# The last recurrence head's stores on GpSimd's queue, eight places for the state's loads, two gates stored as sigmoids, squares in two buffers

## The chip, the cores and the metric

The kernel runs on one core of a Trainium2 chip. A core has four compute engines that the kernel uses side by side: TensorE (PE in the profile, with its weight loads as PEld), VectorE (DVE), ScalarE (ACT) and GpSimd (POOL). A fifth, SyncE (SP), only issues transfers here. Each engine works through its own queue in order, and waits on semaphores where an instruction needs what another engine or a transfer has not yet delivered. The metric is the device time of one execution in microseconds; of several executions the median counts.

## The reference, cut to what matters

One layer of a hybrid backbone over 1024 tokens of width 1024, with 256 context tokens: an adaLN-modulated norm, one combined projection, three token mixers (windowed attention `a`, global attention `b` with normed heads, a bidirectional recurrence `c`), each lifted to the model's width and merged by sigmoid gates, an output projection, and a gated MLP with a depthwise convolution.

```python
aq, ak, av, bq, bk, bv, cq, cf, cb, ci, cg, gates = jnp.split(h @ w_in, split_at, axis=-1)
...
bq = rms_norm(heads(bq, B_HEADS), qn)          # squares, sums, pow(-0.5)
bk = rms_norm(heads(bk, B_KV_HEADS), kn)
...
def merge_branches(ya, yb, yc, gates, w_branch, w_out):
    B_, L = ya.shape[:2]
    ys = jnp.stack([ya, yb, yc], axis=2)
    up = jnp.einsum('blnw,nwd->blnd', ys, w_branch)
    g = jax.nn.sigmoid(gates.reshape(B_, L, N_BRANCH, -1))
    return jnp.sum(g * up, axis=2) @ w_out
```

## The kernel before

All matmuls run on operands that are split into a high and a low part: a product is three matmuls (high by high, high by low, low by high, in an order that each line fixes). ACT casts the high part (`wh`, `T1h`), and DVE subtracts it to get the low part (`wl`, `T1l`). Weights pass through three buffers each of `wr`, `wh` and `wl`.

**Order.** A scheduler places the instructions of each engine, by the order of the program and by priorities (`tc.high_priority`, with an offset for weights and for some steps). What stands ahead of what on an engine is fixed when the program is built. A tile of a pool with one or a few buffers waits for the release of what lay there before.

**The stages that the change touches, in order of time:**

- *The recurrence's last head.* `hgrn_head` is run for four heads. Its `norm` (L1512) squares the head's output on ACT, sums on DVE, takes the power on GpSimd (L1519), and leaves a `turn` (L1522) for later, which transposes (L1525), multiplies by the output gate into `ys` (L1527) and stores it to `y_d` (L1529).
- *The first three gates.* `gate_unit` (L569) multiplies a gate's weights with the state `H` (24 matmuls of 128x512 for each half), copies the result to a tile on ACT (L585) and stores it to `gate_d` (L586). The list `gates` begins with (2,0), (2,1), (1,7). The first runs in the recurrence's pool and calls the two late turns; the other two run in the pool `p3`, in tiles of tag `c` (five buffers, L658).
- *`h_sums` (L660).* It reads the normed state back from `h_d` in eight loads of 512 KB (L666) into `c` tiles, forms four differences on DVE (L669) and splits each into high and low: `T1` to `T4`. A pair of products is then computed with seven block products instead of eight (`pair`, L705): `q0` on a quarter of `H`, `q1` on `T1`, `q2` on `T2`, `q3` on a quarter of `H`, `q4` on `T3`, `q5` on a quarter, `q6` on `T4`. The weights of `q1` to `q4` are sums that DVE makes (L722).
- *Token pairs and gate groups.* `tok_pair` (L840) computes two projections in token-major order, 48 matmuls of 128x256 for each block product; `gate_group` (L751) does four gates, 24 matmuls of 128x512 for each. Two PSUM tiles alternate between the block products; ACT drains `q0`, `q1`, `q2` and `q6` by copies (L870, L780), DVE adds `q3` and `q4` (L785, L875). The elementwise work on a finished projection is queued in `behind` and is called between later matmuls: for branch `b` a square on ACT (L822), a sum on DVE (L824), a scaling (L825), a power on GpSimd (L826), a product (L827), and the rotation (L805 to L810).
- *Attention's end and the merge.* Attention's last steps are matmuls, exponentials on ACT (L1779) and splits (L1664, L1665). `merge_up` (L1794) then makes three passes over the branches (`j` = 0, 1, 2 for `c`, `a`, `b`), eight units `i` each: 24 matmuls (L192 to L194) into `br`, a load of the gate `sgt` (L1822), a sigmoid on ACT (L1823), and the product and sum on DVE (L1826 to L1837). The first units of pass 0 (br20, br21) are placed into attention's end. In passes 1 and 2 a generator `mod_rest` (L593) adds one step to each unit: a load of 512 KB of `w_mod` into a single buffer (L599) and a multiply-add on DVE (L603); after eight of them it transposes the sum (L609, `pm`) and reduces it. The output projection (`wo_half`) follows with the same kind of step.

Names in the profile: `tmt` a token pair's PSUM tile, `g` a gate group's, `ct` and `cg` what they are drained into, `ch` a tile of `h_sums`, `st`, `sg` and `wr` raw weights and their sums, `xm` the merged result, `macc` the sum of `mod_rest`, `wmr` its load.

## Time and profile before

| what | us |
|---|---|
| median of three runs (lowest to highest) | 2078.73 (2076.67 to 2080.57) |
| the profiled execution's own time | 2079.55 |
| its span in the profile | 2077.8 |
| PE busy in the span | 2019.6 |
| DVE, ACT and POOL busy | 1500.8, 1042.1 and 260.4 |
| granted TensorE clock, mean | 0.990 |

The span begins with the program's first instruction and ends with its last; 1.75 us of the execution lie around it. A row of the timeline names the start, the time, the engine, the line, the operation, what it writes and reads, its shape and how many alike are merged; brackets at the end give how long the engine had been idle just before, and what released it. A row of the waits names who waited for whom, the sum, how many times, and the longest.

### The profile page before, as it was taken

To read this page: it belongs to the slowest core of one execution; us is meant where nothing else is said; L and a number is where in the kernel's file an instruction comes from. 1 tells how busy PE (TensorE), PEld (TensorE's weight loads), DVE (VectorE), ACT (ScalarE), POOL (GpSimd) and SP (SyncE) were. 2 spreads that over 40 slices of the span, in tenths; PEclk is the share of its full clock that TensorE was granted. 3 is DMA by queue.
4 is the path that set the end of the run, shared out by engine and by line. 5 is a ranking of instruction groups with operands and counts; after the bars stand their busy time and mean duration, and the time that the engine had idled before them with its cause. 6 is when DMAs were issued, how large, how long until landed. Compare 5 with 4: busy or idle time off the path is not lost.

```text
span 2077.8 us, 29535 instructions
## 1 busy us (share of the span) xinstructions
PE 2019.6 (97%) x11309; PEld 1683.9 (81%) x11309; DVE 1500.8 (72%) x2268; ACT 1042.1 (50%) x1749; POOL 260.4 (13%) x229
## 2 busy tenths in 40 slices
PE   8999999979999999999999899999999999999997
PEld 5888888869897788878888688788888888888886
DVE  3846656665756788678888757898767777779964
ACT  3533323332233877688887733346444544444442
POOL 0000000000011222100000000010333244300001
PEclk9999999989999999999999999999999999999998
DMA  9610111154535211211100475782222222268722
GB/s 370 220 46 31 42 51 33 50 177 131 179 115 181 87 55 54 81 45 32 36 24 24 142 244 194 234 292 87 88 82 82 86 77 82 90 227 307 257 69 82
DMA packets 121790, 248.62 MB, mean 120 GB/s; under 512 B 10608, under 2 KB 51440, under 8 KB 120624
## 3 DMA queue, kind: packets, MB, share of 16 engines
q1 hardware_dynamic: 121552, 246.47, 35.8%
q8 instruction: 89, 1.46, 0.3%
q14 instruction: 53, 0.43, 0.1%
q0 software_dynamic: 96, 0.26, 0.0%
HBM read 196.88 MB, written 49.81 MB: 119 GB/s over the span
## 4 chain that ended last, share of the span: by engine, by line
PE 61%; DVE 3%; DMA 2%; ACT 2%; issue 1%; POOL 0%; SPq 0%; DVEq 0%; POOLq 0%; ACTq 0%
PE pp L1660 5%; PE dn L1252 3%; PE dn L1254 3%; PE dn L1253 3%; PE po L1646 3%; PE po L1647 3%; PE up L1117 3%; PE up L1119 2%; PE up L1118 2%; PE gz L193 2%; PE gz L192 2%; PE gz L194 2%; PE upc L1119 2%; PE upc L1118 2%; PE upc L1117 2%; PE upd L1119 2%
## 5 line engine op out<-in xcount | busy, mean ns | idle before, releaser
L1665 DVE TENSOR_TENSOR pl<-pp,ph 128x512 fp32r<-128x512 f32 x236 | 159.3, 688 | 27.8 <-ACT ph L1664 23.3
L168 ACT CAST wh<-wr 128x1024 fp32r<-128x1024 f32 x71 | 74.6, 1051 | 188.1 <-PE wo L193 33.8
L1664 ACT CAST ph<-pp 128x512 fp32r<-128x512 f32 x236 | 135.2, 588 | 31.8 <-PE pp L1660 29.6
L169 DVE TENSOR_TENSOR wl<-wr,wh 128x1024 fp32r<-128x1024 f32 x71 | 88.1, 1240 | 78.4 <-ACT wh L168 77.7
L1252 PE MATMUL dn<-ac,wh 128*128 128x512 f32 (+2 forms) x311 | 119.3, 384 | 1.3 <-DVE xt L1260 1.2
L1253 PE MATMUL dn<-ac,wh 128*128 128x512 f32 (+2 forms) x311 | 119.3, 384 | 0.5 <-DVE ac L640 0.5
L1254 PE MATMUL dn<-ac,wl 128*128 128x512 f32 (+2 forms) x311 | 119.1, 383 | 0.0
L1646 PE MATMUL po<-ph,VHL 128*128 128x512 f32 x236 | 105.3, 446 | 1.1 <-ACT ph L1664 0.8
L192 PE MATMUL gz<-hh,wh 128*128 128x512 f32 x256 | 103.9, 406 | 0.5 <-ACT gs L585 0.5
L194 PE MATMUL gz<-hh,wl 128*128 128x512 f32 x256 | 102.5, 400 | 0.0
L193 PE MATMUL gz<-hl,wh 128*128 128x512 f32 x256 | 101.5, 397 | 0.0
L1647 PE MATMUL po<-pl,VHL 128*128 128x512 f32 x236 | 98.9, 419 | 0.0
L192 PE MATMUL br<-yh,wh 128*128 128x512 f32 x192 | 76.1, 398 | 3.4 <-DVE xm L1826 3.4
L639 ACT CAST wh<-wr 128x1024 fp32r<-128x1024 f32 (+1 forms) x38 | 38.6, 1018 | 79.5 <-issue 24.8
L1660 PE MATMUL pp<-ident,plat 128*128 128x128 f32 x512 | 77.1, 274 | 0.2 <-DVE pl L1665 0.2
L193 PE MATMUL br<-yl,wh 128*128 128x512 f32 x192 | 76.3, 398 | 0.4 <-DVE yl L1807 0.4
L999 ACT ACTIVATE u<-c,cw 128x1024 f32<-128x1024 f32 x38 | 47.3, 1246 | 58.0 <-DVE c L1154 30.0
L1660 PEld LDWEIGHTS pp<-ident,plat 128*128 128x128 f32 x512 | 62.3, 141 | 16.9 <-DVE pl L1665 2.3
L194 PE MATMUL br<-yh,wl 128*128 128x512 f32 x192 | 75.5, 395 | 0.0
L640 DVE TENSOR_TENSOR wl<-wr,wh 128x1024 fp32r<-128x1024 f32 (+1 forms) x38 | 44.7, 1178 | 41.9 <-ACT wh L639 41.9
L1252 PEld LDWEIGHTS dn<-ac,wh 128*128 128x128 f32 x311 | 58.4, 188 | 13.0 <-DVE xt L1260 1.0
L1253 PEld LDWEIGHTS dn<-ac,wh 128*128 128x128 f32 x311 | 58.4, 188 | 12.2 <-DVE ac L640 1.0
(1538 smaller groups left out, 6318.2 us busy)
## 6 DMA issues: line engine op xcount, KB each, us to landing
wr<-in_w_up SPq DMA_DIRECT2D x44, 512.0 KB, 3.6
wr<-in_w_cm SPq DMA_DIRECT2D x40, 512.0 KB, 3.8
wmr<-in_w_mod SPq DMA_DIRECT2D x32, 512.0 KB, 4.7
wr<-in_w_dn SPq DMA_DIRECT2D x30, 512.0 KB, 4.4
b<-act_d SPq DMA_DIRECT2D x25, 512.0 KB, 6.2
sgt<-gate_d SPq DMA_DIRECT2D x24, 512.0 KB, 4.4
wr<-in_w_tm SPq DMA_DIRECT2D x23, 512.0 KB, 3.7
act_d<-u SPq DMA_DIRECT2D x22, 512.0 KB, 2.6
```

The source lines that it names most:

```text
L192: T.matmul(psl, wh[:, k, c], hh[:, k0 + k, cols], start=s, stop=False)
L193: T.matmul(psl, wh[:, k, c], hl[:, k0 + k, cols], start=False, stop=False)
L194: T.matmul(psl, wl[:, k, c], hh[:, k0 + k, cols], start=False, stop=e)
L1119: T.matmul(psl, w[1][:, c], h[0][:, k], start=False, stop=e, **on)
L1252: T.matmul(z, w[0][:, c], h[0], start=s, stop=False, **on)
L1253: T.matmul(z, w[0][:, c], h[1], start=False, stop=False, **on)
L1254: T.matmul(z, w[1][:, c], h[0], start=False, stop=e, **on)
L1646: T.matmul(po, vv, ph, start=n == 0, stop=False)
L1647: T.matmul(po, vv, pl, start=False, stop=n == len(kts) - 1)
L1660: T.transpose(pp[:, h], PT(h, n), ident)
L1664: A.copy(ph, pp)
L1665: V.tensor_tensor(out=pl, in0=pp, in1=ph.bitcast(F32), op=ALU.subtract)
```

## The change

Five things, in one diff:

1. `gate_unit` takes a place, an issuer and a function. The first gate (2,0) goes to a tile of the recurrence's pool (tag F1), (2,1) and (1,7) to the tags `hsq` and `cs` of `p3`, each of one buffer. The three gates' six stores, and the last head's two `y_d` stores, are issued by GpSimd. Gates (2,0) and (2,1) are stored as sigmoids.
2. `h_sums` reads into eight separate places: five `c` tiles and the tags `t12`, `tbk` and `tbq`. On SP's queue no store stands between its loads any more: after `st02`'s load come ch000, ch010, ch002, ch012, ch110, ch112, ch100 and ch102 in a row, and the rotation's table `cs` behind them. Before, the two `y_d` stores stood ahead of `st02`, and gate stores, weight loads and the table among the eight.
3. The squares of branch `b` alternate between the buffers `hsq` and `cs`.
4. In the merge, `mod_rest` yields once more before its transposes.
5. The first two units of the merge (br20, br21) multiply by the stored sigmoid without an ACT step, and that product has a higher priority. The ACT program then has one table load at the first remaining sigmoid, where it had three.

```diff
-        def gate_unit(pool, n, i, mode, whole=None):
+        def gate_unit(pool, n, i, mode, place=None, by=SP, func=None):
...
-                gs = whole[:, hf] if whole is not None else pool.tile([P, 512], F32, tag="gs", name=f"gs{n}{i}{hf}", bufs=2)
-                A.copy(gs, z)
-                SP.dma_start(gate_d[n, i][:, hf * 512:hf * 512 + 512], gs)
+                if place is None or isinstance(place, tuple):
+                    gs = pool.tile([P, 512], F32, name=f"gs{n}{i}{hf}",
+                                   **(dict(tag=place[hf], bufs=1) if place else dict(tag="gs", bufs=2)))
+                else:
+                    gs = place[:, 0, hf * 512:hf * 512 + 512]
+                if func is None:
+                    A.copy(gs, z)
+                else:
+                    A.activation(gs, z, func)
+                by.dma_start(gate_d[n, i][:, hf * 512:hf * 512 + 512], gs)
...
-        def mod_rest(pool, js, bufs):
+        def mod_rest(pool, js, bufs, gap=False):
...
+                if gap:
+                    yield
                 for hf in range(2):
                     pm2 = bank("a", f"pm2{j}{hf}")
...
-            for j, _ in enumerate(gate_unit(c1, *gates[0], "mm")):
+            for j, _ in enumerate(gate_unit(c1, *gates[0], "mm", c1.tile([P, 2, L], F32, tag="F1", name="g0"), G, AF.Sigmoid)):
...
-                    f[a, b, k] = ctile(f"h{a}{b}{k}")
+                    if (a, b) == (1, 1) or a == 0 and b * k != 2:
+                        f[a, b, k] = ctile(f"h{a}{b}{k}")
+                    else:
+                        f[a, b, k] = p3.tile([P, 2, 512], F32, name=f"ch{a}{b}{k}", bufs=1,
+                                             tag={(1, 2): "t12", (0, 0): "tbk", (0, 2): "tbq"}[b, k])
...
-                for _ in gate_unit(p3, *gates[x], "mm", ctile(f"g{x}")):
+                for _ in gate_unit(p3, *gates[x], "mm", ("hsq", "cs"), G, AF.Sigmoid if x == 1 else None):
...
-                        sq = p3.tile([P, nb, nh, 64], F32, tag="hsq", name=f"hsq{nm}", bufs=1)
+                        sq = p3.tile([P, nb, nh, 64], F32, tag="cs" if u < 2 and t // nb % 2 else "hsq",
+                                     name=f"hsq{nm}", bufs=1)
...
-            merge_up(tc, nc, mp, ins, gate_d, y_d, xm, half, w_unit, gemm_cm, mm2, mod_rest(mq, (0, 1), 1))
+            merge_up(tc, nc, mp, ins, gate_d, y_d, xm, half, w_unit, gemm_cm, mm2, mod_rest(mq, (0, 1), 1, True))
...
-            SP.dma_start(y_d[2, h][:, sl], ys)
+            (G if h == CH - 1 else SP).dma_start(y_d[2, h][:, sl], ys)
...
+                lead = j == 0 and i < 2
                 s = mp.tile([P, L], F32, tag="sgt", name=f"sgt{n}{i}")
                 SP.dma_start(s, gate_d[n, i])
-                A.activation(s, s, AF.Sigmoid)
+                if not lead:
+                    A.activation(s, s, AF.Sigmoid)
                 zf = z.rearrange("p a b -> p (a b)")
                 if j == 0:
-                    V.tensor_tensor(out=mg[i], in0=zf, in1=s, op=ALU.mult)
+                    with tc.high_priority(offset=YPRIO if lead else 0):
+                        V.tensor_tensor(out=mg[i], in0=zf, in1=s, op=ALU.mult)
```

The scheduler's order changes with it. First place: DVE, in the first token pair, around the low half of `q2`'s weights, `wl45` (`wl43` belongs to `q1`, `wl47` to `q3`). Before:

```order
L640 TENSOR_TENSOR wl43_3683<-st02_3621,wh43_3682 128x1024
L669 TENSOR_TENSOR ch000_3577<-ch010_3579,ch000_3577 128x1024
L722 TENSOR_TENSOR st02_3621<-st02_3621,wr44_3736 128x1024
L640 TENSOR_TENSOR T1l_3456<-ch000_3577,T1h_3455 128x1024
L722 TENSOR_TENSOR wr46_3793<-wr46_3793,st02_3621 128x1024
L640 TENSOR_TENSOR wl45_3740<-st02_3621,wh45_3739 128x1024
```

Of the change, the last twelve rows up to the one behind `wl45`; `wl43` stands six rows above the first of them, and the five between are T1l, ch002, st02, ch000 and T1l:

```order
L686 TENSOR_TENSOR ch010_3583<-ch110_3595,ch010_3583 128x1024
L649 TENSOR_TENSOR T2l_3449<-ch000_3581,T2h_3448 128x1024
L686 TENSOR_TENSOR ch002_3588<-ch112_3603,ch002_3588 128x1024
L649 TENSOR_TENSOR T3l_3453<-ch010_3583,T3h_3452 128x1024
L686 TENSOR_TENSOR ch012_3590<-ch112_3603,ch012_3590 128x1024
L649 TENSOR_TENSOR T2l_3449<-ch002_3588,T2h_3448 128x1024
L686 TENSOR_TENSOR ch000_3581<-ch100_3611,ch000_3581 128x1024
L649 TENSOR_TENSOR T3l_3453<-ch012_3590,T3h_3452 128x1024
L686 TENSOR_TENSOR ch002_3588<-ch102_3616,ch002_3588 128x1024
L649 TENSOR_TENSOR T4l_3455<-ch000_3581,T4h_3454 128x1024
L649 TENSOR_TENSOR wl45_3744<-st02_3625,wh45_3743 128x1024
L649 TENSOR_TENSOR T4l_3455<-ch002_3588,T4h_3454 128x1024
```

`wl45` was the fifth operation after `wl43`; now it is the sixteenth, behind all of `h_sums` but the last step.

Second place: ACT, in the second gate group, around the copies that drain its PSUM tiles (`cg26` from `g260` and `g261`, for `q0`, `q1` and `q2` in this order) and the squares `hsq`. Before:

```order
L822 ACTIVATE hsq102_5247<-ct1011_4805 128x512
L780 COPY cg2611_5259<-g260_5201 128x1024
L639 CAST wh103_5361<-wr102_5357 128x1024
L822 ACTIVATE hsq110_5296<-ct1021_5199 128x512
L780 COPY cg2622_5308<-g261_5202 128x1024
L639 CAST wh105_5395<-sg26_5203 128x1024
L639 CAST wh107_5428<-wr106_5425 128x1024
L822 ACTIVATE hsq112_5330<-ct1021_5199 128x512
L780 COPY cg2612_5355<-g260_5201 128x1024
```

And of the change:

```order
L840 ACTIVATE hsq110_5300<-ct1021_5203 128x512
L797 COPY cg2611_5263<-g260_5205 128x1024
L648 CAST wh103_5365<-wr102_5361 128x1024
L840 ACTIVATE hsq112_5334<-ct1021_5203 128x512
L797 COPY cg2622_5312<-g261_5206 128x1024
L648 CAST wh105_5399<-sg26_5207 128x1024
L648 CAST wh107_5432<-wr106_5429 128x1024
L797 COPY cg2612_5359<-g260_5205 128x1024
```

Each square has moved up by one place: a drain that followed one square now follows the next, and the last drain, `cg2612`, has none ahead of it.

Third place: DVE, at the beginning of the merge, around the first products `xm0` and `xm1` (`wl126` is the low half of a later unit's weights). Before:

```order
L169 TENSOR_TENSOR wl126_11883<-wr126_11880,wh126_11882 128x1024
L1826 TENSOR_TENSOR xm0_11650<-br20_11694,sgt20_11719 128x1024
L1826 TENSOR_TENSOR xm1_11651<-br21_11723,sgt21_11748 128x1024
L601 TENSOR_SCALAR macc0_11999<-wmr00_12000,scc_83 128x1024
L1826 TENSOR_TENSOR xm2_11652<-br22_11758,sgt22_11783 128x1024
```

And of the change:

```order
L1847 TENSOR_TENSOR xm0_11654<-br20_11698,sgt20_11723 128x1024
L1847 TENSOR_TENSOR xm1_11655<-br21_11726,sgt21_11751 128x1024
L169 TENSOR_TENSOR wl126_11885<-wr126_11882,wh126_11884 128x1024
L608 TENSOR_SCALAR macc0_12001<-wmr00_12002,scc_83 128x1024
L1847 TENSOR_TENSOR xm2_11656<-br22_11760,sgt22_11785 128x1024
```

The two products stand ahead of `wl126`, which waits for a cast that waits for br21's last matmul. Further on, DVE's order in the first and second pass keeps its shape: `macc0`'s sixth step stands ahead of `yl02`, `xm7` and `yl03` (low halves of branch `a`'s input), in both kernels.

More of the change, by code (lines that the diff above doesn't have):

```diff
@@ L654, in build @@
             hb = {(a, b): [p[:, a * KQ:(a + 1) * KQ, (t1, t2)[b]] for p in H] for a in range(2) for b in range(2)}
-            ht = {n: [hs_.tile([P, KQ, LH], F32R, tag=f"T{n}{p}", name=f"T{n}{p}") for p in "hl"] for n in (4, 3, 2, 1)}
+            ht = {n: [hs_.tile([P, KQ, LH], F32R, tag=f"T{n}{p}", name=f"T{n}{p}") for p in "hl"] for n in (2, 1, 3, 4)}
+            p3.tile([P, 512], F32, tag="hsq", name="hsq", bufs=1)
+            p3.tile([P, 512], F32, tag="cs", name="cs0", bufs=1)
+            p3.tile([P, 1024], F32, tag="s", name="s0", bufs=1)
             def ctile(nm):
```

## The prediction

> **What bounds the kernel now.** I read the page's first part, then PE's waits, then timelines and windows around the longest of them.
>
> ```profile
> span 2077.8 us, 29535 instructions
> ...
> PE 2019.6 (97%) x11309; PEld 1683.9 (81%) x11309; DVE 1500.8 (72%) x2268; ACT 1042.1 (50%) x1749; POOL 260.4 (13%) x229
> ```
>
> ```profile
> PE tmt L861 <- ACT ct L870: 9.8, 1, 9.8
> ...
> PE g L770 <- ACT cg L780: 4.3, 2, 3.7
> PE br L192 <- DVE xm L1826: 3.4, 1, 3.4
> ...
> PE sbl L1772 <- ACT plat L1779: 2.1, 1, 2.1
> PE pm L609 <- DVE macc L603: 1.8, 1, 1.8
> ...
> PE tmt L861 <- ACT T1h L639: 1.5, 1, 1.5
> ...
> PE br L193 <- DVE yl L1807: 0.4, 1, 0.4
> ```
>
> PE is the bound: all its idle time is 58 us. The change goes at five waits of this list: 9.8 and 1.5 (first token pair), 4.3 (second gate group), 2.1 (attention's end), 3.4 and 1.8 (merge). What each is worth depends on what is late next there, so I go through the stages in order, against the profiled execution (2079.55 us: the span and 1.75 us around it). It lies 0.8 above the median of the three runs shown.
>
> **First token pair.**
>
> ```profile
> 430.15 1.73 SPq L666 DMA_DIRECT2D ch<-h_d  x3
> ...
> 454.48 2.72 SPq L666 DMA_DIRECT2D ch<-h_d  x2
> ...
> 460.57 0.36 SPq L666 DMA_DIRECT2D ch<-h_d  x1
> ```
>
> ```profile
> 464.26 1.01 ACT L870 COPY ct<-tmt 128x1024 f32<-128x1024 f32 x1
> ```
>
> ```profile
> 439.85 0.28 PE L861 MATMUL tmt<-wh,hh 128*128 128x256 f32 x1
> ...
> 465.32 0.58 PE L861 MATMUL tmt<-wh,T2h 128*128 128x256 f32 x1 [9.76 <-ACT ct L870]
> ...
> 472.88 0.28 PE L861 MATMUL tmt<-wh,hh 128*128 128x256 f32 x1
> ...
> 478.64 0.28 PE L861 MATMUL tmt<-wh,T3h 128*128 128x256 f32 x1
> ```
>
> These are the starts of q0, q2, q3 and q4. The last h_d load is issued at 460.57; ACT's casts wait for such loads, and the copy that frees q2's PSUM tile stands behind them. An undisturbed product takes 478.64 - 472.88 = 5.76 us; q2 took 7.56, so the clock that was low after the long wait cost 1.8. Without any wait q4 would start at 439.85 + 4 x 5.76 = 462.9, which is 15.8 earlier.
>
> With eight places, and without stores ahead of them, the loads are no longer what is late: in the new order they are out by the time at which the first one goes out now, some 430. Late next is DVE.
>
> ```profile
> 435.46 1.23 DVE L640 TENSOR_TENSOR wl<-st,wh 128x1024 fp32r<-128x1024 f32 x1 [1.42 <-ACT wh L639]
> ...
> 442.56 1.22 DVE L640 TENSOR_TENSOR wl<-st,wh 128x1024 fp32r<-128x1024 f32 x1
> ...
> 463.19 1.22 DVE L640 TENSOR_TENSOR T2l<-ch,T2h 128x1024 fp32r<-128x1024 f32 x1
> 464.33 1.22 DVE L640 TENSOR_TENSOR T3l<-ch,T3h 128x1024 fp32r<-128x1024 f32 x1
> ```
>
> The first row is wl43, the second wl45. Such operations follow each other every 1.14 us (last two rows). wl43 waits for a cast that waits for PE, so I leave it at 435.46. wl45 is now the sixteenth behind it: start 435.46 + 16 x 1.14 = 453.7, end 454.9. q2 starts at 439.85 + 2 x 5.76 = 451.4, and its second matmul needs wl45: **a new wait of 3.5 us**. With the same 1.8 for the clock, q2 ends at 451.4 + 3.5 + 1.8 + 5.8 = 462.4, q3 at 468.2: q4 starts 10.4 earlier. The bounds are 15.8 (no new wait) and 6 (loads that land 4 us too late for DVE push wl45 by as much). I take **-10.4**.
>
> The Trainium skill ("TensorE: Matmul & The Clock Gate", Part 1, "What's actually happening") says that TensorE falls to half rate after an idle window of about 3.4 us and returns after a busy one. By that rule the new wait lies at the edge, and the estimate from the page is -10.4 or, without a slow phase, -12.2; the window quoted below for attention's end shows a low clock already after a wait of 2.1.
>
> The eight stores that go to GpSimd I cost at nothing.
>
> ```profile
> y_d<-yT POOLq DMA_DIRECT2D x2, 128.0 KB, 2.3
> ```
>
> Landing is 2.3 us there, for smaller stores. POOL's short powers for the last head stand between them, and PE waits for the second of those; if a store's issue does hold one up, it costs at most that landing time, once (0 to 2.3).
>
> **Second gate group.**
>
> ```profile
> 639.91 0.63 ACT L822 ACTIVATE hsq<-ct 128x512 f32<-128x512 f32 x1 [3.88 <-DVE hrs L824]
> 640.45 0.99 ACT L780 COPY cg<-g 128x1024 f32<-128x1024 f32 x1
> ```
>
> ```profile
> 641.49 0.80 PE L770 MATMUL g<-T3h,wh 128*128 128x512 f32 x1 [3.69 <-ACT cg L780]
> ```
>
> ```profile
> 649.50 0.39 PE L770 MATMUL g26c<-hh,wh 128*128 128x512 f32 x1
> ```
>
> ```profile
> 654.94 0.39 PE L770 MATMUL g<-T4h,wh 128*128 128x512 f32 x1
> ```
>
> ```profile
> 643.51 0.69 DVE L827 TENSOR_TENSOR ct<-ct,hrs 128x512 f32<-128x512 f32 x1 [1.23 <-POOL hrs L826]
> ...
> 652.00 1.22 DVE L785 TENSOR_TENSOR cg<-g,cg 128x1024 f32<-128x1024 f32 x1
> ```
>
> The PE rows are the starts of q4, q5 and q6. The drain of q2 waits behind a square, that waits for a sum on DVE. The new ACT order has no square ahead of this drain, so the 3.7 goes; the 0.6 of the other drain stays, because the square that now stands ahead of it waits for the same sum as the one before. A product takes 654.94 - 649.50 = 5.44 here, and q4 took 8.01: 2.6 for the clock goes too. But q6 needs the PSUM tile that DVE frees by the add of q4, which ends at 653.2, and DVE gets no faster: it is busy or waits for powers on GpSimd (1.2 at 643.5), not for the squares. q4 at 637.5, q5 at 643, q6 ready at 648.4, and it waits until 653.3: 1.6 earlier than now, with a wait of 4.9 and a slow phase of 2.6 behind it. **Net +0.9** (from -1.6 without the slow phase to +1.3). The wait moves, and the gain doesn't come.
>
> **Attention's end.**
>
> ```profile
> 1155.53 1.28 ACT L1823 ACT_TABLE_LOAD   x1
> ...
> 1159.20 1.11 ACT L1779 ACTIVATE plat<-sbl,st__11329 128x1024 f32<-128x1024 f32 x1
> ```
>
> ```profile
> 1160.00:1165.00 5.00, 4.31 (x14) 3.33 (x15) 3.62 (x6) 5.00 (x14) 0.00 (x0) 0.71 0.64 210
> ```
>
> From 1155.53 to 1159.20 ACT did two table loads and a sigmoid ahead of the exponential; they go. That takes PE's wait of 2.1, and (1 - 0.71) x 5 = 1.5 of low clock behind it. But ACT had no free time in this window (5.00 of 5) and DVE little (3.62); I give back the second part: **-2.1** (0 to -3.6).
>
> **Merge, first products.**
>
> ```profile
> 1191.03 1.23 DVE L169 TENSOR_TENSOR wl<-wr,wh 128x1024 fp32r<-128x1024 f32 x1 [2.15 <-ACT wh L168]
> 1192.29 2.36 DVE L1826 TENSOR_TENSOR xm<-br,sgt 128x1024 f32<-128x1024 f32 x2
> ```
>
> ```profile
> 1195.00:1200.00 5.00, 5.00 (x14) 3.88 (x13) 0.31 (x1) 1.13 (x2) 0.00 (x0) 0.53 0.94 315
> ```
>
> xm0 frees br22's PSUM tile, and stood behind wl126, whose cast waits for PE. Ahead of it xm0 is done long before br22: the 3.4 goes, and the low clock, (1 - 0.53) x 5 = 2.4 in this window and some 0.6 in the 1.4 us before it. **-6.4** (-3.4 to -6.4). The step `pm`, one unit later, no longer meets its multiply-add: **-1.8** (0 to -1.8).
>
> **What the merge and the output projection give back.**
>
> ```profile
> 1227.96 1.28 DVE L603 SCALAR_TENSOR_TENSOR macc<-wmr,scc,macc 128x1024 f32<-128x1024 f32 x1 [2.76 <-DMA wmr<-in_w_mod]
> ```
>
> ```profile
> 1285.27 1.28 DVE L603 SCALAR_TENSOR_TENSOR macc<-wmr,scc,macc 128x1024 f32<-128x1024 f32 x1
> ...
> 1313.71 1.28 DVE L603 SCALAR_TENSOR_TENSOR macc<-wmr,scc,macc 128x1024 f32<-128x1024 f32 x1
> ```
>
> ```profile
> wmr<-in_w_mod SPq DMA_DIRECT2D x32, 512.0 KB, 4.7
> ```
>
> A step of `mod_rest` is a multiply-add of 1.28 and a load of 4.7 into the same buffer: 6.0 us, where PE's unit takes 5.44. At 1227.96 such a step makes DVE wait 2.8 for its load, and yl02, xm7 and yl03 stand behind it; PE already waits 0.4 for them (last row of the second fence). The chain's start moves up too, but not quite as far as PE: give back 1. In the third pass DVE needs (1313.71 - 1285.27) / 5 = 5.69 for a unit: 8 x 0.25 = 2. In the output projection eight more steps could cost 8 x 0.55 = 4.4, and a slow phase of 2.6 if that comes in one wait: 0 to 7, and I take the middle, 3.5. **+6.5** (0 to 10).
>
> **Sum.** -10.4 + 0.9 - 2.1 - 6.4 - 1.8 + 6.5 = -13.3, and 2079.55 - 13.3 = 2066.3 us.
>
> **The rivals.**
>
> - *Every wait that is removed stays removed.* -15.8 - (3.7 + 2.6) - 3.6 - 6.4 - 1.8 = -33.9: 2045.7. The list of waits speaks for it; against it, wl45's place on DVE and the end of q4's add at 653.2, which no part of the change moves. Chance 0.04.
> - *The merge keeps what it wins* (no give-back): 2059.8, with the range 2057 to 2062. For it: DVE's wait for the load at 1227.96 shrinks if the chain starts with PE. Chance 0.20.
> - *The first pair doesn't do what it says.* Eight loads of 512 KB in one burst share what three shared; if the last land after 451 (when the fourteenth operation behind wl43 needs it), wl45 goes with them, and the part is worth 4 instead of 10.4: 2072.7 (2071 to 2075). Against it: some 20 us lie between issue and need. Chance 0.14.
> - *The `w_mod` chain becomes the bound: slower than before.* The gap sets the second sum's steps one unit later against PE, and PE comes earlier. Of 32 steps, each that costs 6.0 + x beyond PE's 5.44 is paid in full once the chain decides. The parts ahead win 19.8 in all; 32 x (6.0 - 5.44 + x) passes that from x = 0.06, a load of 4.8 instead of 4.7, if all 32 decided; if half did, from x = 0.7, a load of 5.4. With half the steps and a load of 5.7 it would be 2079.55 - 19.8 + 16 x 1.56 = 2084.7. Against it: DVE waits for such loads at only some of the steps, and pass 0 needs none. Chance of slower 0.04; of a result near zero by the same mechanism, or by the last two rivals together, 0.08 (2075 to 2082).
>
> **How the numbers follow.** The forecast, 2062 to 2071 around 2066.3, has 0.50. Faster by over 0.2% (below 2074.6; that is about what a measurement of this kernel can tell from no change): 0.50 + 0.20 + 0.04 + 0.14 = 0.88. Within 0.2%: 0.08. Slower: 0.04. The range leaves out the first rival, half of the near-zero cases and the slower ones: 2057 to 2077.
>
> **What would show it.** In the profile after: no wait of `tmt` for the drain `ct` around 450, but one of L862 for wl45 of 3 to 4 us (a shorter one: the loads or wl43 came earlier; a wait for an h_d load: third rival). In the second gate group no wait for `cg` over 1 us, and one of some 5 us ahead of q6 for DVE's add. `plat` and `xm` gone from PE's waits. Several waits under 1.5 us in passes 1 and 2, for `yl`, `sgt` or casts behind DVE, in place of the 1.8. If those are absent, the second rival is right; if PE waits for `macc`'s neighbours at each unit, the last one. The forecast is wrong in kind if q4 of the first pair starts less than 6 us earlier, or if the gate group's new wait is missing.

## The result, and the profile after

| | before | changed |
|---|---|---|
| median of four runs, us (lowest to highest) | 2079.65 (2076.67 to 2081.13) | 2066.47 (2065.21 to 2066.99) |
| the profiled execution's own time | 2079.55 | 2066.99 |

The ratio is 0.9938, with a 95% interval from 0.9925 to 0.9952. The forecast was 2066.3, 13.3 below the profiled execution of before; the profiled execution of the changed kernel is 12.6 below it. Total and forecast agree, but one term was too large, one reason was wrong, and both need the experiments.

The first part of the changed kernel's page:

```profile
span 2065.2 us, 29550 instructions
...
PE 2014.6 (98%) x11309; PEld 1679.2 (81%) x11309; DVE 1500.9 (73%) x2268; ACT 1036.9 (50%) x1745; POOL 267.0 (13%) x237
```

The rows of PE's waits that answer to those of before:

```profile
PE g L787 <- DVE cg L802: 4.6, 1, 4.6
PE tmt L880 <- DVE wl L649: 3.3, 1, 3.3
PE rpm L262 <- POOL rsm L252: 3.1, 2, 2.3
...
PE br L192 <- DVE sgt L1855: 1.7, 2, 1.3
PE wo L192 <- ACT B21h L1857: 1.3, 1, 1.3
PE gz L192 <- ACT gs L590: 1.2, 2, 0.7
...
PE g L787 <- ACT cg L797: 0.6, 1, 0.6
```

The 9.8 for `ct` and the 1.5 for `T1h` are gone, and a wait of 3.3 for wl45 has come. The 3.7 for `cg` on ACT is gone, and 4.6 for `cg` on DVE has come. `plat`, `xm` and `pm` are gone. New and small are `sgt`, `B21h`, a wait of 0.9 for `mods`, and more of `rpm` (1.3 before), all from the merge's third pass on, and more of `gs` (0.5 before), which no step of the prediction had.

Nearly every reading below goes by stages. The table has the start of q0 (the first token pair's first matmul), and the length of four stages between starts in PE's timeline: q0 to q4 of the first pair; the second gate group's first matmul to that of the next gate; from there to br00, the merge's second pass; from br00 to the start of the output projection's last product. The ratio stands against the kernel before in the same session.

| run | median | ratio (95%) | q0 at | q0 to q4 | gate group | to br00 | br00 to projection's end |
|---|---|---|---|---|---|---|---|
| before | 2079.65 | | 439.85 | 38.79 | 45.40 | 568.84 | 177.30 |
| changed | 2066.47 | 0.9938 (0.9925 to 0.9952) | 440.94 | 29.11 | 46.04 | 559.98 | 181.68 |
| e1 stores on SP | 2068.81 | 0.9958 (0.9946 to 0.9970) | 440.28 | 32.41 | 46.08 | 560.52 | 180.98 |
| e2 five places | 2066.65 | 0.9948 (0.9936 to 0.9960) | 440.73 | 29.58 | 45.54 | 559.65 | 180.95 |
| e3 one square buffer | 2064.28 | 0.9940 (0.9928 to 0.9953) | 440.94 | 28.01 | 43.94 | 559.59 | 182.46 |
| e4 no gap | 2061.14 | 0.9922 (0.9910 to 0.9933) | 441.59 | 28.07 | 46.12 | 559.50 | 176.70 |
| e5 no lead | 2073.09 | 0.9971 (0.9962 to 0.9980) | 441.57 | 27.84 | 45.27 | 566.50 | 180.77 |
| e6 half loads | 2067.77 | 0.9949 (0.9937 to 0.9962) | 441.67 | 28.08 | 45.56 | 560.01 | 181.85 |
| e7 wl45 first | 2063.03 | 0.9926 (0.9913 to 0.9939) | 441.35 | 24.27 | 46.44 | 560.20 | 181.64 |
| e8 other tile | 2065.77 | 0.9938 (0.9925 to 0.9952) | 441.17 | 28.08 | 40.95 | 564.00 | 181.04 |
| e9 gap, second sum | 2061.67 | 0.9931 (0.9918 to 0.9943) | 441.01 | 27.88 | 45.27 | 559.49 | 178.23 |
| e10 own place | 2064.53 | 0.9943 (0.9930 to 0.9955) | 439.89 | 28.34 | 45.52 | 560.57 | 180.62 |
| e11 three edits | 2056.88 | 0.9906 (0.9890 to 0.9921) | 441.60 | 24.27 | 44.31 | 559.32 | 177.78 |
| e12 late transposes | 2052.74 | 0.9882 (0.9866 to 0.9898) | 439.95 | 24.68 | 45.66 | 558.48 | 176.10 |

Two cautions. The median of the kernel before lay between 2075.68 and 2079.65 in the five sessions, and a ratio's interval is some 0.0013 wide to either side, 2.7 us; smaller differences between kernels are read from the stages. And a stage of one profiled execution moves too: the first pair takes 27.8 to 28.1 us in the six kernels that leave it alone (e3 to e6, e8, e9), and 29.1 in the changed kernel itself. Below about 1 us a single stage says nothing.

### The profile page after: what moved, and what is told of

It is laid out like the page before. It is cut to its first block, busy times and chain, and to the rows that moved or that the text cites. A ratio compares the mean times of both kernels' runs of the same rounds, so it can differ in the third digit from the quotient of the medians.

```text
span 2065.2 us, 29550 instructions
## 1 busy us (share of the span) xinstructions
PE 2014.6 (98%) x11309; PEld 1679.2 (81%) x11309; DVE 1500.9 (73%) x2268; ACT 1036.9 (50%) x1745; POOL 267.0 (13%) x237
## 4 chain that ended last, share of the span: by engine, by line
PE 57%; DVE 3%; DMA 3%; issue 3%; ACT 2%; POOL 0%; SPq 0%; DVEq 0%; ACTq 0%; POOLq 0%
PE pp L1678 5%; PE dn L1270 3%; PE dn L1272 3%; PE dn L1271 3%; PE po L1664 3%; PE po L1665 3%; PE up L1135 3%; PE up L1136 3%; PE up L1137 3%; PE gz L193 2%; PE gz L192 2%; PE gz L194 2%; PE upc L1136 2%; PE upc L1137 2%; PE upc L1135 2%
```

## Experiments

All start from the changed kernel. They keep two pieces of the change that the diff as printed above leaves out, another order in which the tiles of `T1` to `T4` are laid out and three tiles of `p3` that are reserved early; no run undoes these. In the expectations of e1 and e7 the 464.3 is the start of q3; q4 starts at 470.05.

### The first token pair: queue or places?

**e1: the stores go back to SP, the eight places stay.**

```diff
-            for j, _ in enumerate(gate_unit(c1, *gates[0], "mm", c1.tile(...), G, AF.Sigmoid)):
+            for j, _ in enumerate(gate_unit(c1, *gates[0], "mm", c1.tile(...), SP, AF.Sigmoid)):
...
-                for _ in gate_unit(p3, *gates[x], "mm", ("hsq", "cs"), G, ...):
+                for _ in gate_unit(p3, *gates[x], "mm", ("hsq", "cs"), SP, ...):
...
-            (G if h == CH - 1 else SP).dma_start(y_d[2, h][:, sl], ys)
+            SP.dma_start(y_d[2, h][:, sl], ys)
```

> The changed kernel, but SP issues the last head's two stores and the six gate stores again; the eight places stay. Theory A (in SP's queue a store that waits for its data holds up the h_d loads behind it): the last h_d load goes out 5 us or more later than 434.6, q2 or q3 of the first token pair waits for an h_d tile, and q4 starts 2 to 3 us later than the 464.3 of the changed kernel: 2068 to 2069. Theory B (the eight places alone carry the gain of the first pair, and the stores on GpSimd only cost the 1.1 us by which q0 came later): q0 starts at 439.9 again, q4 not later than 464, 2065.4.

**e2: all eight loads pass through the five `c` tiles, the stores stay on GpSimd.**

```diff
-                    if (a, b) == (1, 1) or a == 0 and b * k != 2:
+                    if True:
                         f[a, b, k] = ctile(f"h{a}{b}{k}")
```

> The changed kernel, but all eight h_d loads go through the five c tiles again; the stores stay on GpSimd. Theory A (the places carry the gain): the last three loads wait for a free tile, go out after 450 as in the kernel before, the drain of q0 waits behind their casts, and most of the 8.6 us of the first pair are lost: 2072 to 2075. Theory B (the stores in SP's queue held the loads up, and the places are worth next to nothing): the last three loads go out before 452, q4 starts 0 to 2.5 us later than in the changed kernel: 2066.5 to 2069.

SP's timeline, with the h_d loads: first of the changed kernel, then of e1, then of e2.

```profile
409.95 24.62 SPq L683 DMA_DIRECT2D ch<-h_d  x8
```

```profile
434.36 0.33 SPq L593 DMA_DIRECT2D gate_d<-gs  x1
434.74 0.43 SPq L683 DMA_DIRECT2D ch<-h_d  x1
436.39 0.33 SPq L593 DMA_DIRECT2D gate_d<-gs  x1
436.77 1.59 SPq L683 DMA_DIRECT2D ch<-h_d  x3
441.81 0.33 SPq L593 DMA_DIRECT2D gate_d<-gs  x1
442.26 0.93 SPq L683 DMA_DIRECT2D ch<-h_d  x2
```

```profile
410.65 13.12 SPq L683 DMA_DIRECT2D ch<-h_d  x5
446.19 6.53 SPq L683 DMA_DIRECT2D ch<-h_d  x3
```

A merged row's second number reaches to the last of its instructions: the eight loads are out by 434.6 in the changed kernel, by 443.2 in e1, by 452.7 in e2. In e1 each store that waits for its data holds the loads behind it. The waits for the drain that stands behind the loads' casts on ACT, in e1 and then in e2:

```profile
PE tmt L879 <- ACT ct L888: 2.5, 1, 2.5
```

```profile
PE tmt L879 <- ACT ct L888: 4.4, 1, 4.4
```

e1 went as theory A has it: the stage takes 3.3 us more than in the changed kernel, q0 comes 0.7 earlier, and the ratio is 0.9958 instead of 0.9938 (the two intervals overlap a little). e2 went as theory B has it: a ratio of 0.9948, not to be told from the changed kernel's, and 0.5 us more in the stage. Its 4.4 stands in place of the 3.3 for wl45, it doesn't come on top. So either edit alone brings most of the stage's gain (38.79 to 32.41 by the places, to 29.58 by the stores), together they bring little more than the stores do (29.11, or the 28 of its neighbours), and what then remains is wl45.

**e7: wl45 goes ahead of most of `h_sums` on DVE.**

```diff
-                    with tc.high_priority(offset=wprio[0] + SPRIO):
+                    with tc.high_priority(offset=wprio[0] + SPRIO + (400 if nm == "t02" and q == 2 else 0)):
```

> The changed kernel, but the sum and the split of the third product's weights (wl45) of the first token pair go ahead of most of the sixteen DVE operations of h_sums. Theory A (q2 waits for wl45 alone): the wait of 3.3 us and most of the low clock behind it, 1.8, go; q4 starts near 459.5 instead of 464.3; 2061 to 2062. Theory B (the split parts of T2 or T3, which come out later by these two operations, are late next and take the wait over): q4 starts at 462 or later, 2064 to 2067.

The wait of 3.3 for `wl` is 1.0 in e7, and the stage takes 24.27 instead of 29.11. Theory A by the stage, though a wait of 1.0 for another `wl` remains; the median, 2063.03, lies between the two theories' ranges, and the ratio of 0.9926 goes theory A's way, within its interval. The new wait of the changed kernel is the bound of this stage that the prediction took it for. Its rows, from DVE's timeline, PE's, and the windows (PEclk, the granted clock, is the third number from the right):

```profile
454.77 1.21 DVE L649 TENSOR_TENSOR wl<-st,wh 128x1024 fp32r<-128x1024 f32 x1
```

```profile
456.03 0.58 PE L880 MATMUL tmt<-wl,T2h 128*128 128x256 f32 x1 [3.30 <-DVE wl L649]
```

```profile
455.00:460.00 5.00, 3.97 (x18) 3.97 (x19) 5.00 (x6) 1.04 (x1) 0.00 (x0) 0.50 0.00 0
460.00:465.00 5.00, 5.00 (x37) 5.00 (x36) 4.07 (x5) 1.57 (x2) 0.00 (x0) 0.82 0.79 235
```

**e10: the third gate gets a place of its own.** q0 came 1.1 later than before, and the prediction had nothing there. In PE's and ACT's timelines of the changed kernel:

```profile
435.36 0.50 PE L192 MATMUL gz<-hh,wh 128*128 128x512 f32 x1 [0.74 <-ACT gs L590]
```

```profile
434.73 0.59 ACT L590 COPY gs<-gz 128x512 f32<-128x512 f32 x1 [12.47 <-PE gz L194]
441.62 0.59 ACT L590 COPY gs<-gz 128x512 f32<-128x512 f32 x1 [0.45 <-DMA gate_d<-gs]
```

Gates (2,1) and (1,7) share the places `hsq` and `cs`, one buffer each. A copy of (1,7) can't begin before the store of (2,1) from the same place has landed: the store issued at 428.58 landed after 6.0 us, at 434.62, and the copy began at 434.73. The landing times (kilobytes of one, then the median from issue to landing) of the changed kernel:

```profile
gate_d<-gs SPq DMA_DIRECT2D x26, 256.0 KB, 2.0
...
y_d<-ys SPq DMA_DIRECT2D x6, 256.0 KB, 2.0
gate_d<-gs POOLq DMA_DIRECT2D x4, 256.0 KB, 4.9
gate_d<-g POOLq DMA_DIRECT2D x2, 256.0 KB, 2.5
y_d<-ys POOLq DMA_DIRECT2D x2, 256.0 KB, 6.5
```

```diff
-                for _ in gate_unit(p3, *gates[x], "mm", ("hsq", "cs"), G, ...):
+                for _ in gate_unit(p3, *gates[x], "mm", ("hsq", "cs") if x == 1 else
+                                   p3.tile([P, 1, L], F32, tag="tbq", name="g17", bufs=1), G, ...):
```

> The changed kernel, but the third gate before the first token pair goes into a place of its own (that of the last h_d load, which comes after it) in place of the two that the second gate's stores by GpSimd hold until they have landed. Theory A (the copies of the third gate wait for those stores, which land 4.9 us after their issue, and so q0 starts 1.1 us later than before): PE's wait for gs shrinks below 0.5, q0 starts at 440.0 or earlier, and if the last h_d load does not come too late the time is 0.5 to 1 shorter, 2065.5 to 2066. Theory B (the issue of the stores on GpSimd, 0.6 us each among the last head's powers, delays the head itself): q0 stays at 440.9 or later, 2066.5.

In PE's and ACT's timelines of e10:

```profile
439.89 0.28 PE L879 MATMUL tmt<-wh,hh 128*128 128x256 f32 x1
```

```profile
429.21 0.59 ACT L590 COPY g<-gz 128x512 f32<-128x512 f32 x1 [6.97 <-PE gz L194]
440.29 0.58 ACT L590 COPY g<-gz 128x512 f32<-128x512 f32 x1
```

Theory A: the copy runs at 429.21 instead of 434.73, and q0 is back at 439.89. The column "q0 at" also holds a drift of up to 0.8 us from the program's first part; counted from the first gate's first matmul, q0 comes after 54.3 us in the kernel before, 55.5 in the changed kernel, 54.3 in e1, 54.6 in e2 and 54.5 in e10. The ratio (0.9943) can't show a gain of 1.1 us.

That GpSimd issues these stores explains little of their late landing. In the kernel before, SP issued the same two gates' stores, also among the h_d loads:

```profile
gate_d<-cg SPq DMA_DIRECT2D x4, 256.0 KB, 4.6
```

They took nearly as long, but each gate lay in a `c` tile of its own, so no copy of the next gate waited for them. The cost is that of two shared places beside a burst of loads.

### The second gate group

**e3: one buffer for the squares again.**

```diff
-                        sq = p3.tile([P, nb, nh, 64], F32, tag="cs" if u < 2 and t // nb % 2 else "hsq",
+                        sq = p3.tile([P, nb, nh, 64], F32, tag="hsq",
```

> The changed kernel with one buffer for the squares, as before. Theory A (as predicted: the second buffer moves the wait from q4 to q6, and q6 then waits for the add that ends the tile's use): the wait of 3.7 us for cg on ScalarE is back ahead of q4 of the second gate group, the wait of 4.6 for DVE ahead of q6 is gone, and the time is 0.9 shorter, 2065.6. Theory B (the second buffer is worth its wait, and q6 would wait anyway): 3.8 plus 2.5 us longer, 2073.

The two rows of PE's waits in e3:

```profile
PE g L787 <- ACT cg L797: 4.3, 2, 3.7
...
PE g L787 <- DVE cg L802: 0.7, 1, 0.7
```

Theory A. The waits change places. By the stage, the four kernels with one buffer (before, e3, e11, e12) take 44.8 on the mean (43.9 to 45.7), the nine with two buffers and the old tile 45.8 (45.3 to 46.4): the second buffer costs some 1 us, too little for the ratio (0.9940).

The spread with one buffer is the clock. The same wait of 3.7 stands ahead of q4 in all four kernels, and q4 then took 8.01 us before, 5.58 in e3, 6.91 in e11 and 8.26 in e12, where an undisturbed product takes 5.44. The windows from the wait on, first of the kernel before, then of e3, where the clock did not fall at all:

```profile
640.00:645.00 5.00, 3.51 (x8) 2.84 (x9) 3.77 (x9) 2.38 (x3) 2.21 (x2) 0.50 0.65 209
645.00:650.00 5.00, 5.00 (x20) 4.01 (x19) 4.08 (x7) 0.48 (x1) 1.43 (x1) 0.83 0.03 10
```

```profile
630.00:635.00 5.00, 3.19 (x14) 2.66 (x15) 3.77 (x9) 2.48 (x3) 1.64 (x1) 1.00 0.60 202
635.00:640.00 5.00, 5.00 (x24) 4.15 (x23) 4.08 (x8) 1.06 (x1) 1.65 (x1) 1.00 0.03 11
```

So the price of the second buffer in one execution is uncertain by more than its mean.

**e8: the seventh product goes into the other PSUM tile.** In this kernel the seventh product adds onto the fourth's content instead of the fifth's, so one quarter of each gate group's outputs is not the reference's; the work on PE is the same.

```diff
-                    z_ = z[q % 2 if q < 4 else 0]
+                    z_ = z[(0, 1, 0, 1, 0, 0, 1)[q]]
```

> The changed kernel, but the seventh product of a gate group goes into the PSUM tile that the fourth one's add frees, not the one that the fifth one's add frees; squares in two buffers as in the changed kernel. Theory A (q6 waits only for that add; the two buffers did take the drain's wait away, and the tile gave it back): the wait of 4.6 us ahead of q6 and the slow phase of 2.2 to 2.6 behind it go, 2059.5 to 2061. Theory B (DVE, busy throughout, is late with the weights of q6 or of the next product, and the wait moves once more): less than 3 us, 2063.5 to 2067.

The stage falls to 40.95, by 5.1, as theory A has it: without the add on DVE in its way the gain of the second buffer does come. But the next stage takes 564.00 instead of 559.98. Its longest new wait, in PE's timeline of e8:

```profile
660.75 0.54 PE L1627 MATMUL kt<-identr,qs_kk 128*128 128x128 f32 x4 [2.65 <-ACT qs_kk L1618]
```

Attention's first steps wait for ACT, the granted clock is 0.66 in the 5 us from 660 on, and 4.0 of the 5.1 are gone. Why ACT is late there was not tested. The ratio is that of the changed kernel, 0.9938: theory B. The tile can't be swapped in a kernel that must compute the reference, and it would bring little.

### Attention's end and the merge's first products

**e5: no stored sigmoids, no early order for the first two products.**

```diff
-                lead = j == 0 and i < 2
+                lead = False
```

(and the two gates stored without the sigmoid)

> The changed kernel without the two sigmoids that are stored and without the early order of the first two merge products; the gap stays. Both theories expect the 2.0 us at attention's end and the 7.1 us of the merge's first products to be lost. Theory A (the gap alone gives 4.4 us back, wherever TensorE stands in time): the loss from the merge's second pass to the end of the output projection stays near 4.4, and the time is 9.1 longer than that of the changed kernel, 2075 to 2076. Theory B (as predicted: the steps give back because TensorE comes earlier): with a later TensorE most of the 4.4 is not given back, 2071 to 2072.

The two waits are back in e5:

```profile
PE br L192 <- DVE xm L1847: 3.4, 1, 3.4
...
PE sbl L1790 <- ACT plat L1797: 2.1, 1, 2.1
```

The stage to br00 is 6.5 longer than in the changed kernel, and the ratio 0.9971. That is less than the 8.9 between before and the changed kernel: the first four units of pass 0 took 38.7 us here and 40.3 before, with the same two waits. The 1.6 are the clock: in the two windows of 5 us from the longer wait on it was 0.81 and 0.84 here, 0.79 and 0.53 before, which is 1.8 us lost against 3.4. Of the 4.4 that is given back behind br00, 180.77 - 177.30 = 3.5 remain although PE comes later: theory A by that stage. The median, 2073.09, lies between the two theories' ranges.

### What is given back

**e4: no gap.**

```diff
-            merge_up(tc, nc, mp, ins, gate_d, y_d, xm, half, w_unit, gemm_cm, mm2, mod_rest(mq, (0, 1), 1, True))
+            merge_up(tc, nc, mp, ins, gate_d, y_d, xm, half, w_unit, gemm_cm, mm2, mod_rest(mq, (0, 1), 1))
```

> The changed kernel without the additional yield ahead of the transposes (gap off). Theory A (as predicted: the steps of mod_rest cannot keep up with a TensorE that comes earlier, whatever their place, and the gap saves the wait pm): the wait pm for macc of 1.8 us is back, the merge and the output projection give back as much as now, 2066.5 to 2068.5. Theory B (the gap itself sets the second sum's steps and its transposes one unit later, into the third pass's end, and the waits rpm, br, wo and rcm of the output projection come from that): the gains stay at some 15 us from the merge's second pass to the end of the output projection, 2061.5 to 2063.

Theory B, clearly: 2061.14, where e2, equal to the changed kernel in time, had 2066.65 in the same session (0.9922 against 0.9948), and the last stage takes 176.70, less than before (177.30). The wait that the gap was to save is back, in e4:

```profile
PE pm L618 <- DVE macc L610: 1.7, 1, 1.7
```

PE reaches br00 as early as in the changed kernel, and nothing is given back. An early PE is not the cause.

**e6: each load of `w_mod` in two halves, the gap stays.**

```diff
-                    wm = pool.tile([P, D], F32, tag="wmr", name=f"wmr{j}{k}", bufs=bufs)
+                  for x in range(2 if j < 2 else 1):
+                    n = D // 2 if j < 2 else D
+                    wm = pool.tile([P, n], F32, tag=f"wmr{x}", name=f"wmr{j}{k}{x}", bufs=bufs)
```

> The changed kernel, gap and all, but each w_mod row block of the merge's mod_rest is loaded as two halves into two places of half the size (the same memory), so that one half's load runs beside the other half's multiply-add; 16 more DVE instructions and loads in all, none added to what is computed. Theory A (what decides in a step is the load into the one place, 4.7 us, behind the multiply-add that frees it): the waits sgt, rpm and B21h of the third pass and the output projection shrink, at least the 4.4 us come back, and 2 to 4 us more where DVE stood waiting for the load: 2057 to 2062. Theory B (DVE's own work in the longer row of steps decides, or the transposes' place in TensorE's order): no gain, 2066 to 2069.

No gain at all, theory B: 181.85 for the last stage. A half took 4.0 us to land:

```profile
wmr<-in_w_mod SPq DMA_DIRECT2D x32, 256.0 KB, 4.0
```

That and a multiply-add of 0.75 make 4.75 for a step, less than the unit's 5.44, and still as much was given back. Taken alone the run is weak evidence against the chain of load and multiply-add: in the third pass (1255 to 1306) DVE stood idle for these loads for 3.5 us in all. But in the changed kernel itself that was 1.6 us, so DVE hardly waited for the chain there, and e4 has the same chain.

**e9: the gap only ahead of the second sum's transposes.**

```diff
-                if gap:
+                if gap and j == 1:
```

> The changed kernel with the gap only ahead of the second sum's transposes (before the first sum's the old place). This leaves the second sum's eight multiply-adds where they stood without a gap and moves its transposes and two reductions one unit later. Theory A (the eight multiply-adds that move one unit later, towards the end of the third pass, cost the 4.4): as without any gap, 2060 to 2062, and the wait pm of 1.8 may go as well. Theory B (the transposes and the two reductions behind them, which then stand among the last units' drains on VectorE, cost it): 2064.5 to 2067.

The result is that of theory A, 2061.67 and a last stage of 178.23, but the run tells less than it was meant to: the scheduler put the reductions and the multiply-adds on DVE in the same order as in e4, and PE waits for `pm` as there. It is a second measure of e4.

**e11: one square buffer, no gap and wl45 first, together.** The edits are those of e3, e4 and e7.

> The changed kernel with three of the edits together: one buffer for the squares, no gap, wl45 ahead of h_sums on VectorE. If the three are independent, as their places in the program (first token pair, second gate group, merge) suggest, their gains add: against the changed kernel 3.5 (wl45) + 1 to 2 (one buffer) + 4.4 to 5.3 (no gap): 2054.5 to 2057.5. If the merge's loads or VectorE's order take back what comes earlier, as in the run with the other PSUM tile, 2058 to 2061.

2056.88 and a ratio of 0.9906. By the stages, against the changed kernel, 4.8 + 1.7 + 3.9 us: the three add, as expected for independent places. The profiled executions differ by 10.8. The medians, each against its session's kernel before, give 19.8 - 13.2 = 6.6, and the two intervals leave 2 to 11.

**e12: e11 with the third gate's own place, and with two yields ahead of the second sum's transposes alone.**

```diff
-                if gap:
-                    yield
+                for _ in range(2 * gap * j):
+                    yield
```

> The kernel with three edits (one buffer for the squares, wl45 first, no yield between the two sums' multiply-adds), with two more: the third gate in a place of its own, and two yields ahead of the second sum's transposes alone. So the eight multiply-adds of the second sum stand where they stood without a gap, and the transposes and the two reductions stand in the last unit of the third pass, as in the changed kernel. Theory A (the multiply-adds that moved cost the 4.4): the wait pm is gone or below 0.5, nothing is given back between the third pass and the projection's end, and the time is 1 (own place) and 1 to 2.6 (pm) shorter than with the three edits: 2053.5 to 2055. Theory B (the transposes and the reductions among the last drains cost it): waits for B21h, rcm and rpm come back, 3 us or more are lost from the third pass to the projection's end, 2057 to 2060.

Now the transposes and reductions did move: the transposes stand behind the last unit of the third pass, and the two reductions run 2.1 us after the projection's start (1295.35), as in the changed kernel (2.4 us after 1304.57). In DVE's timeline of e12:

```profile
1290.65 1.28 DVE L610 SCALAR_TENSOR_TENSOR macc<-wmr,scc,macc 128x1024 f32<-128x1024 f32 x1 [0.42 <-DMA wmr<-in_w_mod]
...
1297.43 1.28 DVE L619 TENSOR_REDUCE mods<-pm 128x4 f32<-128x512 f32 x2
```

The wait `pm` is gone, and nothing is given back: the last stage takes 176.10, the shortest of all. So the place of the second sum's transposes costs nothing, and the gap's price is that it also moves the second sum's eight multiply-adds one step of `mod_rest` later. (The gap moves the first sum's transposes too, and no run moves these alone; but from br00 to the third pass the changed kernel takes 44.98 us, where the kernel before takes 45.31, so nothing is lost there.) 2052.74 is 22.9 below the kernel before in its session (2075.68), the ratio is 0.9882 (0.9866 to 0.9898): it beats both kernels.

How that step becomes 4.4 us can be read from the waits, though no run separates them further. In DVE's timeline the last multiply-add, first of the changed kernel, then of e4:

```profile
1300.92 1.28 DVE L610 SCALAR_TENSOR_TENSOR macc<-wmr,scc,macc 128x1024 f32<-128x1024 f32 x1
```

```profile
1295.80 1.28 DVE L610 SCALAR_TENSOR_TENSOR macc<-wmr,scc,macc 128x1024 f32<-128x1024 f32 x1
```

It stands 3.7 us ahead of the projection's start (1304.57) in the changed kernel and 7.5 ahead (1303.31) in e4. DVE, which needed more than a unit's time in this pass (5.69 against 5.44 before), has no free unit left to catch up, and seems to enter the projection late. PE's waits of the changed kernel that come from there are `sgt` 1.7, `B21h` 1.3, and

```profile
PE rcm L241 <- DVE mods L619: 0.9, 1, 0.9
```

and 1.8 more of `rpm` than in e4, which has none of the others above 0.4:

```profile
PE rpm L262 <- POOL rsm L252: 1.3, 2, 0.7
```

1.7 + 1.3 + 0.9 + 1.8 = 5.7, less the 1.7 of `pm`, is 4.0 of the 5.0 between the two last stages.

## Why the prediction was right, and where it was not

- **First token pair, -10.4: measured -8.6.** The mechanism held: no wait for the drain, a new one for wl45, 3.30 long where 3.5 was worked out, with DVE starting wl45 at 454.77 (453.7 worked out) and a low clock behind it. From q0 to q4 the stage is 9.7 shorter. Two terms were mis-sized. The first is "the eight stores that go to GpSimd I cost at nothing": they cost 1.1. The bound of 0 to 2.3 held by luck and by another way than the one named: not GpSimd's powers wait, but the copies of the next gate, for places that the stores hold while they land (e10), and the store in question took 6.0 us to land, not 2.3. The step counted the queue from which the stores were taken and the one that got them, and left out how long their source tile is held beside a burst of loads. The second is the 1.8 for the clock: q2 took 11.84 us, which is 5.76 + 3.30 + 2.8; in e3 to e6, e8 and e9, with the same wait, it was 1.5 to 1.8.
- **Places and stores.** The step named the two causes together. e1 and e2 show that they overlap: with the stores on GpSimd, eight places are worth nothing that can be measured. The third rival (eight loads in one burst come too late) didn't occur.
- **Second gate group, +0.9: measured +0.9** from q4 of the first pair to the next gate (a gain of 8.59 becomes one of 7.65). The wait for `cg` on ACT went from q4 to one of 4.6 on DVE ahead of q6, as worked out (4.9; q4 without its wait should read 641.49 - 3.69 = 637.8 instead of 637.5, which makes it 4.6 and leaves the net as it was). That the net agrees to a tenth is luck: the clock alone moves q4 by over 2 us from one execution to another (e3). e3 shows the price with one buffer, e8 that the add on DVE is what held q6 up.
- **Attention's end -2.1 and the merge's first products -6.4: measured -8.9 together.** Undoing them costs 6.5, with a shorter slow phase than before (e5); the forecast lies between.
- **`pm` -1.8 and the give-back +6.5, net +4.7: measured +4.4.** The size was right: 1 was worked out for the second pass, 2 - 1.8 for the third, 3.5 for the projection; PE's starts (br10 at 1257.69, the projection at 1304.57, against 1274.53 and 1321.22 before) give -0.3, +0.2 and +4.5. The reason was wrong. The step said that a chain of load and multiply-add of 6.0 us cannot follow a PE that comes earlier. e4 has the same early PE and the same chain and gives back nothing; e6 has a shorter chain by its medians and gives back as much; e5 has a later PE and gives back 3.5; and DVE waited only 1.6 us for the chain's loads in the third pass. What stood in its place is the gap: it saves the 1.8, as late transposes alone do, and it costs 5.6 (the last stage takes 181.68, and 176.10 in e12), by moving eight multiply-adds one step towards the projection. So the agreement in size is luck. The last rival named this shift, but only as an aid to an early PE.
- **The rivals.** "The merge keeps what it wins" gave 2059.8; that is what the change does without its gap (2061.1). "Every wait that is removed stays removed" fell at wl45 and at q6's add, the two places that spoke against it; e7 and e8 lift one each.
- **The sum.** -13.3 against -12.6. The first pair was 1.8 too good, the merge's two terms together 0.7 too cautious (-8.9 instead of -8.5, +4.4 instead of +4.7). No large errors of size cancelled; but the give-back came out right for a wrong reason, and a change planned on that reason, as e6 was, gains nothing.

## What to carry to other kernels

When a step is moved, count what it holds, not only what it waits for and who waits behind it: a store holds its tile until it has landed, and beside a burst of loads that was 6 us here and not 2.4. A yield in a generator of filler work moves all the filler behind it; move the instruction that is late, alone, and the wait goes without a price. Where two edits act on one wait, undo each: one of them may carry all of it, and the new wait that takes its place is where the next gain lies.

## What the runs showed of the hardware

- GpSimd's two stores of the first gate (256 KB each) went out ahead of the h_d loads and landed after 2.5 and 2.4 us in the changed kernel. The Trainium skill ("DMA: Bandwidth & Descriptors", "Anatomy of one DMA — SWDGE (gpsimd) path") gives 2.0 us plus the bytes over 436 KB per us for a transfer on GpSimd's path; an estimate from that page is 2.6 us. The two stores agree with it.
- Stores among the h_d loads took longer, whoever issued them: medians of 4.9 and 6.5 us from GpSimd in the changed kernel, 4.6 from SP for the same two gates in the kernel before. The loads make the difference: the last head's first store, issued by GpSimd at 423.7 each time, took 6.9 us in the changed kernel, where five h_d loads went out in the 2.5 us ahead of it, and 2.4 in e10 and e12, where one did.
- The same wait of PE can be followed by a slow phase or by none: after 3.7 us the clock was 0.50 and 0.83 in the kernel before and 1.00 in e3. The wait of 2.6 for `pm` in e11 left it at 1.00, the 3.3 for wl45 was followed by a slow phase in every kernel that had it.
- From 1250 to 1306, loads of 256 KB landed after a median of 4.0 us in e6 and loads of 512 KB after 3.9 in the changed kernel. The halves often went out in pairs, so no run shows a half by itself.
